# Delta-rule chains in four parts per step, and an output projection that starts on its attention half

## The chip, the core and the metric

One core of a Trainium2 chip runs the kernel. The metric is device time in microseconds (us) of one execution; the time of a kernel is the median of several runs. One execution was also taken by the hardware profiler, and every row of a trace below is from it.

## What is computed

The kernel is one encoder block on 1024 tokens plus 16 meta tokens, width 1024. Two head groups work side by side on the same normalised input, and one output projection joins them; an MLP follows. What the change touches is the recurrence of the first group and the join:

```python
def step(S, xs):                                   # per chunk, per direction, 4 heads
    q_i, k_i, u_i, w_i, qk_i, gl_i = xs
    v_new = u_i - einsum('bhck,bhkv->bhcv', w_i, S)
    o_i = einsum('bhck,bhkv->bhcv', q_i, S) + einsum('bhij,bhjv->bhiv', qk_i, v_new)
    S = S * gl_i[..., None, None] + einsum('bhck,bhcv->bhkv', k_i, v_new)
    return S, o_i
...
o = rms_norm(o_f + o_b, o_norm_w) * silu(heads(z))
mix = concatenate([o_dn, o_at], axis=-1) @ w_out[l]
h = h + rms_norm(mix, norm_mix_post[l])
u = rms_norm(h, norm_mlp_pre[l])
f = square(relu(u @ w_up[l])) @ w_down[l]
```

The second group is softmax attention with 8 query heads over all tokens.

## The kernel before

**Stages.** Input projections and the triangular inverses of the delta rule fill the first 400 us. Then three things share the engines: the two chains of the delta rule (one forward, one backward over 8 chunks of 128 tokens, `chain`, L1065), attention (8 tiles of 128 queries, 8 heads each, so 64 heads), and the output projection with its norms (`proj_stream`, L1387, 8 tiles). After that come the MLP's two products, each written as seven products of half-size blocks.

**A chain's step.** For a chunk c and four heads: the state times the keys (`st,KT`), eviction to `rr` on VectorE (DVE, L1078); the inverse times it (`rr,tt`), eviction to `vn`, which is `rr` again (L1090); the queries times the state (`st,QT`), eviction to `O` on ScalarE (ACT, L1097), and for a chunk that the other direction has already visited a sum with its stored output `Oprev` on GpSimd (POOL, L1099); `rr,kd`, whose eviction makes the next state (L1107); and `rr,at`, which DVE adds to `O` (L1113). `Oprev` is loaded from `oscr` in DRAM. The four operands of the next chunk (`vt`, `tt`, `kd`, `at`, 256 KB each) are loaded with `chunk_load` as soon as the step has used the old ones. All matrix products of a chain are float32, 128 x 128.

**A head of attention.** Four products of 512 columns into `S`, a minimum on DVE (L1254), the exponential on ACT (L1262), a cast (L1268) and the rest of the split on POOL and DVE (L1270, L1271) into `P`, one DMA transpose from `P` to `pT` (L1274, 128 x 16 x 128 values of two bytes) issued by SyncE's queue (SP), and 24 products `o<-VP,pT` (27 with a share of the meta tokens). At most six heads are between their scores and their products.

**The projection.** `mix(c)` transposes a tile of attention (`AQ`) and of the delta rule (`on`) and splits both; 96 products follow in the order `WORD`: first the attention rows of the weight (`woah`, `woal`), then the delta rule's (`wobh`, `wobl`). The first four are loaded by `wload_stream`, the others by `wout_stream` (L1334), which has to wait for both chains, because it takes over their memory.

**What sets the order.** Every stream is a Python generator. `progress` (L1538) runs the first stream of the list `URGENCY` whose due time has come on a planned clock, which counts TensorE's columns. After a `yield` a stream is due again its `LAT` later (2.2 us for the chains), or after the number of microseconds that it yields. `need` holds a stream until other streams have set a mark. So a `yield` between two parts of a chain's step puts 2.2 us of other streams' work between them. All this only fixes the order; the Tile framework then lays the instructions out, and each engine runs its own list in order, each instruction with its waits.

Of the kernel before, what the change touches and what calls it, by code (L numbers as in the profile page):

```python
# [13 lines left out]
ALU = mybir.AluOpType  # L14
AX = mybir.AxisListType
P = 128
# [65 lines left out]
def body(tc, I, out, dbg=None):  # L82
# [32 lines left out]
    def psr():  # L115
        return psa.tile([P, 512], F32, name="a", tag="a")
# [10 lines left out]
    def bc(ap, m):  # L127
        return ap.unsqueeze(2).broadcast_to([ap.shape[0], ap.shape[1], m])
# [4 lines left out]
    def v3(ap, m=P):  # L133
        return ap.rearrange("p (h c) -> p h c", c=m)
# [918 lines left out]
    def chunk_load(d, c, names):  # L1053
        if 0 <= c < NT:
            for n_ in names:
                loaded[n_, d] = t = ct_(f"{n_}{d}")
                S.dma_start(t, vscr[c * P:(c + 1) * P, :] if n_ == "vt" else {"at": dscr, "kd": kscr, "tt": tscr}[n_][d * NT + c])

    def ct_(name):

        if name not in R:
            R[name] = R["chn"].tile([P, 512], F32, name=name)
        return R[name]

    def chain(d, c, nxt):  # L1065
        gc = c * 8 + d * 4
        st = state[d]
        QT = R["QT"]
        tt, at, kd, vt = (loaded[n_, d] for n_ in ("tt", "at", "kd", "vt"))
        qc = [QT[:, h, c * P:(c + 1) * P] for h in range(NH)]  # L1070
        first = c not in seen
        seen.add(c)
        ps = psr()
        for h in range(NH):
            T.matmul(v3(ps)[:, h], lhsT=kcol(h, c), rhs=v3(st)[:, h], start=True, stop=True)
        rr = ct_(f"rr{d}")
        for h in range(NH):
            V.scalar_tensor_tensor(v3(rr)[:, h], v3(ps)[:, h], Egc[:, d, c, h:h + 1], v3(vt)[:, h], ALU.mult, ALU.subtract)  # L1078
        yield
        chunk_load(d, nxt, ("vt",))  # L1080
        if not first:
            yield from need(f"o{c}")
            prev = ct_(f"Oprev{d}")
            S.dma_start(prev, oscr[c])
        yield
        ps = psr()
        for h in range(NH):
            T.matmul(v3(ps)[:, h], lhsT=v3(tt)[:, h], rhs=v3(rr)[:, h], start=True, stop=True)
        vn = rr
        V.tensor_tensor(v3(vn), v3(ps), bc(nbeta[:, gc:gc + 4], P), ALU.mult)  # L1090
        yield
        ps = psr()
        for h in range(NH):
            T.matmul(v3(ps)[:, h], lhsT=qc[h], rhs=v3(st)[:, h], start=True, stop=True)
        oq = ct_(f"O{d}")
        for h in range(NH):
            A.activation(v3(oq)[:, h], v3(ps)[:, h], AF.Copy, scale=Egc[:, d, c, h:h + 1])  # L1097
        if not first:
            G.tensor_tensor(oq, oq, prev, ALU.add)  # L1099
        chunk_load(d, nxt, ("tt",))  # L1100
        yield
        ps = psr()
        for h in range(NH):
            T.matmul(v3(ps)[:, h], lhsT=v3(kd)[:, h], rhs=v3(vn)[:, h], start=True, stop=True)
        sg = ct_(f"st{d}{nxt % 2}")
        for h in range(NH):
            V.scalar_tensor_tensor(v3(sg)[:, h], v3(st)[:, h], Egl[:, d, c, h:h + 1], v3(ps)[:, h], ALU.mult, ALU.add)  # L1107
        state[d] = sg
        yield
        ps = psr()  # L1110
        for h in range(NH):
            T.matmul(v3(ps)[:, h], lhsT=v3(at)[:, h], rhs=v3(vn)[:, h], start=True, stop=True)
        V.tensor_tensor(oq, oq, ps, ALU.add)  # L1113
        chunk_load(d, nxt, ("kd",))
        yield
        chunk_load(d, nxt, ("at",))
        if first:
            S.dma_start(oscr[c], oq)
            mark(f"o{c}", 2.0)
            return  # L1120
        so = small(NH, "so", 2)
        jk = junk()
        for h in range(NH):
            A.activation(jk[:, :P], v3(oq)[:, h], AF.Square, accum_out=so[:, h:h + 1])
        mo = small(NH, "mo", 2)
        V.tensor_scalar(mo, ssq[:, c], P * EPS, P * EPS * EPS, ALU.mult, ALU.add)
        V.scalar_tensor_tensor(mo, so, 1.0 / P, mo, ALU.mult, ALU.add)
        ro = small(NH, "ro", 2)
        G.tensor_tensor(ro, mo, mhalf[:, :NH], ALU.pow)
        G.tensor_tensor(v3(oq), v3(oq), bc(ro, P), ALU.mult)  # L1130
        yield
        S.dma_start(oscr[c], oq)
# [193 lines left out]
    def wout_raw(k, r):  # L1326
        S.dma_start(r, w_out[k * P:(k + 1) * P, :])
        return r
# [5 lines left out]
    def wout_stream():  # L1334
        yield from need("chain0", "chain1", "wload")
        right.close()
        rkt.close()
        w3 = R["w3"] = pool(right, "w3", 2, side="right")
        wob = [w3.tile([P, 4, D], F32R, name=n, bufs=1) for n in ("wobh", "wobl")]
        R["npost"] = w3.tile([P, D], F32, name="npost", bufs=1)  # L1340
        R["npre"] = w3.tile([P, D], F32, name="npre", bufs=1)
        R["dnw"] = w3.tile([P, 1], F32, name="dnw", bufs=1)
        raw = [wout_raw(k, R[("npost", "npre")[k]] if k < 2 else tmp()[:, :D]) for k in range(4)]
        yield 4.0
        for k in range(4):
            wout_split(wob[0][:, k], wob[1][:, k], raw[k])
            yield
        R["wout"] = {k: tuple(a[:, k % 4] for a in (wob, R["wo"])[k // 4]) for k in range(KD)}
        S.dma_start(R["dnw"], I["dn_out_norm"][0].rearrange("(p o) -> p o", o=1))
        S.dma_start(R["npost"], I["norm_mix_post"][0].partition_broadcast(P))  # L1350
        S.dma_start(R["npre"], I["norm_mlp_pre"][0].partition_broadcast(P))
        mark("wout", 2.0)
        yield 4.0
        mx, su, isu = (w3.tile([P, 1], F32, name=n, bufs=1) for n in ("gmx", "gsu", "isu0"))
        R["isu"] = isu
        V.tensor_reduce(mx, R["npre"], AX.X, ALU.max, apply_absolute_value=True)
        V.tensor_scalar(mx, mx, 1e-30, None, ALU.max)
        pow2_below(mx, isu, su, 2.0 ** 7)
        V.tensor_scalar(R["npre"], R["npre"], su[:, 0:1], None, ALU.mult)
        mark("gain", 1.0)  # L1360
# [3 lines left out]
    def mix(c):  # L1364
# [19 lines left out]
        V.tensor_tensor(ml[:, 0:4], on, mh[:, 0:4].bitcast(F32), ALU.subtract)  # L1384
        return mh, ml

    def proj_stream():  # L1387
        mixes = {}
        yield from need("wout", "att0")
        mixes[0] = mix(0)  # L1390
        yield
        wout, npost = R["wout"], R["npost"]
        for c in range(NT):
            if c + 1 < NT:
                yield from need(f"att{c + 1}")
# [6 lines left out]
            for n in range(2):  # L1402
                sl = slice(n * 512, (n + 1) * 512)
                pso.append(psr())
                yield from mm3(pso[n], [(mh[:, k], ml[:, k], wout[k][0][:, sl], wout[k][1][:, sl]) for k in WORD], 2)
                A.activation(junk()[:, sl], pso[n], AF.Square, accum_out=s2[:, n:n + 1])
                yield
            rs = small(1, "rs")
# [482 lines left out]
```

## Time and profile before

| | us |
|---|---|
| median of 3 runs (1413.14 to 1415.83) | 1415.37 |
| the profiled execution, its own time | 1416.07 |
| its span, first to last instruction | 1414.2 |
| PE busy (TensorE's products), share of the span | 1342.7, 95% |
| DVE busy | 1029.3, 73% |
| ACT busy | 835.5, 59% |
| POOL busy | 295.4, 21% |
| mean granted clock of TensorE, as a share of 2.4 GHz | 0.979 |

PE is TensorE, PEld its weight loads. A busy share of 95% says little by itself, since a product counts as busy from its issue to its modelled end and these overlap; the profile has to be read stage by stage. The profile's second part, the span in 40 slices, shows PE below nine tenths only between some 400 and 810 us, and there the DMA engines are at nine tenths or more for most of the slices. That is the stage of chains, attention and projection. Rows with "<-" name what an engine waited for; "SPq" is SyncE's queue, which issues nearly all DMAs.

### The profile page before, as it was taken

Reading aid. Unit: us, or ns where it says so; the run is one execution under the profiler, and the core shown is the slowest. Engines: PE = TensorE matmul, PEld = TensorE weight load, DVE = VectorE, ACT = ScalarE, POOL = GpSimd, SP = SyncE. Lnnn points to the kernel's source line nnn. Section 1 sums busy time; section 2 is a strip of 40 time slices with the busy share of each in tenths; the row PEclk is TensorE's granted clock in tenths of the full one; section 3 lists DMA queues with packets and bytes.
Section 4 is the critical chain, followed back from the end, with each engine's and each line's share of the span. In section 5 each row is a group of like instructions: output and inputs, shape, how many; then the busy total and the mean of one; then the engine's idle time right before and its main releaser. Section 6 shows DMA issues by size and latency. Waiting matters only on the chain. (4 is left out here: it accounts for less than half of the span.)

```text
span 1414.2 us, 26476 instructions
## 1 busy us (share of the span) xinstructions
PE 1342.7 (95%) x9627; PEld 1027.1 (73%) x9627; DVE 1029.3 (73%) x1962; ACT 835.5 (59%) x1747; POOL 295.4 (21%) x386
## 2 busy tenths in 40 slices
PE   6999999999998998899998799999999999999996
PEld 6999888777998877677777444444444888888875
DVE  5636779788768979877765987777775588675675
ACT  6556565756546777866644676666665455445552
POOL 1210234343534456533321200000000000000000
PEclk9999999999998999889999799999999999999998
DMA  6312234344379999997994354444443984466341
GB/s 209 87 57 62 83 98 158 112 149 153 121 253 282 245 264 239 221 242 186 224 225 135 102 175 158 153 155 150 158 155 114 331 271 127 142 193 194 98 150 66
DMA packets 273355, 236.86 MB, mean 167 GB/s; under 512 B 147484, under 2 KB 201656, under 8 KB 273224
## 3 DMA queue, kind: packets, MB, share of 16 engines
q1 hardware_dynamic: 270056, 225.73, 55.3%
q10 hardware_dynamic: 3168, 9.44, 1.8%
q8 instruction: 76, 1.25, 0.4%
q14 instruction: 55, 0.45, 0.1%
HBM read 132.27 MB, written 69.28 MB: 143 GB/s over the span
## 5 line engine op out<-in xcount | busy, mean ns | idle before, releaser
L95 PEld LDWEIGHTS <-wh 128*128 128x128 f16 x896 | 88.1, 99 | 102.7 <-issue 1.9
L95 PE MATMUL a<-woah 128*128 128x512 f32 x672 | 158.6, 390 | 1.3 <-DVE woah L1734 1.2
L95 PE MATMUL a<-woal 128*128 128x512 f32 x672 | 157.4, 389 | 0.0
L95 PEld LDWEIGHTS a<-woah 128*128 128x128 f32 x672 | 125.9, 188 | 29.0 <-DVE woah L1734 2.0
L95 PEld LDWEIGHTS a<-woal 128*128 128x128 f32 x672 | 126.1, 188 | 26.2
L95 PE MATMUL a<-uh,wh 128*128 128x344 f32 (+2 forms) x340 | 122.3, 360 | 0.7 <-ACT cw L665 0.5
L1270 POOL TENSOR_TENSOR P<-t,P 128x640 f16<-128x640 f32 x64 | 99.4, 1555 | 106.8 <-ACT P L1268 85.0
L95 PE MATMUL a<-ul,wh 128*128 128x344 f32 (+2 forms) x340 | 118.7, 349 | 0.5 <-DVE ul L262 0.5
L95 PE MATMUL a<-uh,wl 128*128 128x344 f32 (+2 forms) x340 | 118.3, 348 | 0.0
L161 POOL TENSOR_TENSOR rs<-ms,mhalf 128x1 f32<-128x1 f32 (+1 forms) x33 | 19.1, 578 | 424.0 <-DVE rs L1797 304.6
L1254 DVE TENSOR_REDUCE mx<-S 128x1 f32<-128x1024 f32 x64 | 77.9, 1219 | 24.3 <-PE S L95 24.1
L1262 ACT ACTIVATE t<-S,nb 128x1024 f32<-128x1024 f32 x64 | 71.5, 1117 | 40.8 <-DVE nb L1255 29.2
L95 PEld LDWEIGHTS <-pT 128*128 128x128 f16 x1536 | 59.5, 100 | 42.0 <-issue 26.6
L95 PE MATMUL o<-VP,pT 128*128 128x65 f16 (+1 forms) x1536 | 73.6, 198 | 11.3 <-DMA pT<-P 9.8
L95 PEld LDWEIGHTS <-wl 128*128 128x128 f16 x448 | 43.9, 98 | 54.1 <-issue 1.7
L1731 ACT ACTIVATE woah<-fr,isf 128x512 fp32r<-128x512 f32 x54 | 39.2, 725 | 70.3 <-PE a L95 61.0
L1731 ACT ACTIVATE woal<-fr,isf 128x512 fp32r<-128x512 f32 x54 | 39.2, 726 | 68.4 <-PE a L95 66.2
L1268 ACT CAST P<-t 128x1024 f16<-128x1024 f32 x64 | 66.8, 1043 | 4.7 <-DVE t L269 1.8
L1733 DVE SCALAR_TENSOR_TENSOR woah<-fr,isf,woah 128x512 fp32r<-128x512 f32 x54 | 40.5, 751 | 37.2 <-ACT woah L1731 37.1
L95 PE MATMUL S<-KH,qs 128*128 128x512 f32 x128 | 61.0, 476 | 6.5 <-ACT t L1262 6.5
L95 PEld LDWEIGHTS a<-uh,wh 128*128 128x128 f32 x340 | 65.0, 191 | 2.5 <-ACT cw L665 0.7
L95 PEld LDWEIGHTS a<-ul,wh 128*128 128x128 f32 x340 | 65.1, 192 | 2.1 <-DVE ul L262 1.0
(508 smaller groups left out, 3776.8 us busy)
## 6 DMA issues: line engine op xcount, KB each, us to landing
fr<-fscr SPq DMA_DIRECT2D x108, 256.0 KB
fscr<-os SPq DMA_DIRECT2D x64, 256.0 KB
rb<-in_w_down SPq DMA_DIRECT2D x64, 256.0 KB
fscr<-of SPq DMA_DIRECT2D x48, 256.0 KB
wr<-in_w_in SPq DMA_DIRECT2D x44, 256.0 KB
AQ<-in_w_up SPq DMA_DIRECT2D x22, 512.0 KB
raw<-in_w_up SPq DMA_DIRECT2D x10, 512.0 KB
X<-in_x SPq DMA_DIRECT2D x8, 512.0 KB
```

Source lines behind the costliest of these rows:

```text
L95: nc.tensor.matmul(out, lhsT=lhsT, rhs=rhs, **kw)
L161: G.tensor_tensor(dst, ms[:r, :n], mhalf[:r, :n], ALU.pow)
L1254: V.tensor_reduce(mx, s, AX.X, ALU.min)
L1262: A.activation(p32[:, :L], s, AF.Exp, bias=nb, scale=-1.0)
L1268: A.copy(p16[:, 0], p32[:, :L])
L1270: G.tensor_tensor(p16[:, 1, :LH], p32[:, :LH], p16[:, 0, :LH], ALU.subtract)
L1731: A.activation(ah, fr, AF.Copy, scale=isf[:, p:p + 1])
L1733: V.scalar_tensor_tensor(al, fr, isf[:, p:p + 1], ah.bitcast(F32), ALU.mult, ALU.subtract)
```

## The change

It does three things. A chain's step has two `yield`s fewer: the one behind the loads of the first part and the one ahead of the last part's loads are gone, so that a step has four parts, `KT`, `tt`, `kd` with `QT`, and `at` (a chunk's second visit has a fifth, its norm). The product with the queries moves behind the state's update, into the same part. The loads move with them: `tt` and `kd` are now issued in the part that has used them, and `Oprev` is asked for after `vn` and no longer after `rr`. And the output projection waits at first for `w3` only (the weights' pool is open and their loads are issued), and for `wout` ahead of the delta rule's half of the products.

```diff
--- before.py
+++ after.py
@@ -1076,19 +1076,27 @@
         rr = ct_(f"rr{d}")
         for h in range(NH):
             V.scalar_tensor_tensor(v3(rr)[:, h], v3(ps)[:, h], Egc[:, d, c, h:h + 1], v3(vt)[:, h], ALU.mult, ALU.subtract)
-        yield
         chunk_load(d, nxt, ("vt",))
-        if not first:
-            yield from need(f"o{c}")
-            prev = ct_(f"Oprev{d}")
-            S.dma_start(prev, oscr[c])
         yield
         ps = psr()
         for h in range(NH):
             T.matmul(v3(ps)[:, h], lhsT=v3(tt)[:, h], rhs=v3(rr)[:, h], start=True, stop=True)
         vn = rr
         V.tensor_tensor(v3(vn), v3(ps), bc(nbeta[:, gc:gc + 4], P), ALU.mult)
-        yield
+        chunk_load(d, nxt, ("tt",))
+        if not first:
+            yield from need(f"o{c}")
+            prev = ct_(f"Oprev{d}")
+            S.dma_start(prev, oscr[c])
+        yield
+        ps = psr()
+        for h in range(NH):
+            T.matmul(v3(ps)[:, h], lhsT=v3(kd)[:, h], rhs=v3(vn)[:, h], start=True, stop=True)
+        sg = ct_(f"st{d}{nxt % 2}")
+        for h in range(NH):
+            V.scalar_tensor_tensor(v3(sg)[:, h], v3(st)[:, h], Egl[:, d, c, h:h + 1], v3(ps)[:, h], ALU.mult, ALU.add)
+        state[d] = sg
+        chunk_load(d, nxt, ("kd",))
         ps = psr()
         for h in range(NH):
             T.matmul(v3(ps)[:, h], lhsT=qc[h], rhs=v3(st)[:, h], start=True, stop=True)
@@ -1097,22 +1105,11 @@
             A.activation(v3(oq)[:, h], v3(ps)[:, h], AF.Copy, scale=Egc[:, d, c, h:h + 1])
         if not first:
             G.tensor_tensor(oq, oq, prev, ALU.add)
-        chunk_load(d, nxt, ("tt",))
-        yield
-        ps = psr()
-        for h in range(NH):
-            T.matmul(v3(ps)[:, h], lhsT=v3(kd)[:, h], rhs=v3(vn)[:, h], start=True, stop=True)
-        sg = ct_(f"st{d}{nxt % 2}")
-        for h in range(NH):
-            V.scalar_tensor_tensor(v3(sg)[:, h], v3(st)[:, h], Egl[:, d, c, h:h + 1], v3(ps)[:, h], ALU.mult, ALU.add)
-        state[d] = sg
         yield
         ps = psr()
         for h in range(NH):
             T.matmul(v3(ps)[:, h], lhsT=v3(at)[:, h], rhs=v3(vn)[:, h], start=True, stop=True)
         V.tensor_tensor(oq, oq, ps, ALU.add)
-        chunk_load(d, nxt, ("kd",))
-        yield
         chunk_load(d, nxt, ("at",))
         if first:
             S.dma_start(oscr[c], oq)
@@ -1340,13 +1337,14 @@
         R["npost"] = w3.tile([P, D], F32, name="npost", bufs=1)
         R["npre"] = w3.tile([P, D], F32, name="npre", bufs=1)
         R["dnw"] = w3.tile([P, 1], F32, name="dnw", bufs=1)
+        R["wout"] = {k: tuple(a[:, k % 4] for a in (wob, R["wo"])[k // 4]) for k in range(KD)}
+        S.dma_start(R["dnw"], I["dn_out_norm"][0].rearrange("(p o) -> p o", o=1))
         raw = [wout_raw(k, R[("npost", "npre")[k]] if k < 2 else tmp()[:, :D]) for k in range(4)]
+        mark("w3")
         yield 4.0
         for k in range(4):
             wout_split(wob[0][:, k], wob[1][:, k], raw[k])
             yield
-        R["wout"] = {k: tuple(a[:, k % 4] for a in (wob, R["wo"])[k // 4]) for k in range(KD)}
-        S.dma_start(R["dnw"], I["dn_out_norm"][0].rearrange("(p o) -> p o", o=1))
         S.dma_start(R["npost"], I["norm_mix_post"][0].partition_broadcast(P))
         S.dma_start(R["npre"], I["norm_mlp_pre"][0].partition_broadcast(P))
         mark("wout", 2.0)
@@ -1384,12 +1382,23 @@
         V.tensor_tensor(ml[:, 0:4], on, mh[:, 0:4].bitcast(F32), ALU.subtract)
         return mh, ml
 
+    def proj_mm(ps, mh, ml, sl):
+
+        for i, k in enumerate(WORD):
+            if i == 4:
+                yield from need("wout")
+            wh, wl = (w[:, sl] for w in R["wout"][k])
+            for j, (a, b) in enumerate(((mh, wh), (mh, wl), (ml, wh))):
+                T.matmul(ps, lhsT=a[:, k], rhs=b, start=i == 0 and j == 0, stop=i == KD - 1 and j == 2)
+            if i % 2 and i + 1 < KD:
+                yield
+
     def proj_stream():
         mixes = {}
-        yield from need("wout", "att0")
+        yield from need("w3", "att0")
         mixes[0] = mix(0)
         yield
-        wout, npost = R["wout"], R["npost"]
+        npost = R["npost"]
         for c in range(NT):
             if c + 1 < NT:
                 yield from need(f"att{c + 1}")
@@ -1402,7 +1411,7 @@
             for n in range(2):
                 sl = slice(n * 512, (n + 1) * 512)
                 pso.append(psr())
-                yield from mm3(pso[n], [(mh[:, k], ml[:, k], wout[k][0][:, sl], wout[k][1][:, sl]) for k in WORD], 2)
+                yield from proj_mm(pso[n], mh, ml, sl)
                 A.activation(junk()[:, sl], pso[n], AF.Square, accum_out=s2[:, n:n + 1])
                 yield
             rs = small(1, "rs")
```

**On TensorE, chains.** The chains' second step before and third step with the change, in both the place where the last input projections run out (`st` is a state, `rr` with `tt`, `kd`, `at` the other products, `idr`, `KM` the first query tile; forward and backward have different numbers). Before:

```order
L95 MATMUL a<-rr_5956,tt_5764 128x128 x4
L95 MATMUL a<-rr_5966,tt_5774 128x128 x4
L95 MATMUL a<-idr,t_6263 128x128 x8
L95 MATMUL a<-st_6153,QT 128x128 x4
L95 MATMUL a<-st_6163,QT 128x128 x4
L95 MATMUL a<-KM,qs 128x32 x8
L95 MATMUL a<-rr_5956,kd_5766 128x128 x4
L95 MATMUL a<-rr_5966,kd_5776 128x128 x4
```

With the change:

```order
L95 MATMUL a<-rr_5956,tt_5764 128x128 x4
L95 MATMUL a<-rr_5967,tt_5774 128x128 x4
L95 MATMUL a<-rr_5956,kd_5766 128x128 x4
L95 MATMUL a<-st_5758,QT 128x128 x4
L95 MATMUL a<-rr_5967,kd_5776 128x128 x4
L95 MATMUL a<-st_5768,QT 128x128 x4
L95 MATMUL a<-rr_5956,at_5762 128x128 x4
L95 MATMUL a<-st_6060,KT 128x128 x4
L95 MATMUL a<-rr_5967,at_5772 128x128 x4
L95 MATMUL a<-st_6081,KT 128x128 x4
```

The chains' products now follow each other with nothing between them; `kd` stands right behind `tt` and `QT` behind `kd`. Over the whole stage the two lists, counted in products, compare as follows:

| in TensorE's list, counted from the chains' first product | before | change |
|---|---|---|
| products up to the chains' last one | 1429 | 661 |
| of these, heads' scores / heads' products with `pT` | 35 / 29 | 12 / 6 |
| from there to the projection's first product | 369 | 376 |
| heads' scores / heads' products still to come at that point | 18.5 / 24.0 | 41.5 / 46.8 |
| products of the projection after the last head's | 96 | 91 |

**On SyncE's queue, the end of the chains.** Before, from the last chain stores on:

```order
L1132 DMA oscr<-O_6109 128x512
L1327 DMA t_8730<-in_w_out 128x1024
L1327 DMA t_8732<-in_w_out 128x1024
L1327 DMA npost<-in_w_out 128x1024
L1327 DMA npre<-in_w_out 128x1024
L1274 DMA_TRANSPOSE pT<-P_6215 128x16x128
L1274 DMA_TRANSPOSE pT<-P_6216 128x16x128
```

With the change:

```order
L1129 DMA oscr<-O_6092 128x512
L1324 DMA t_7512<-in_w_out 128x1024
L1271 DMA_TRANSPOSE pT<-P_6380 128x16x128
L1341 DMA dnw<-in_dn_out_norm 128x1
L1324 DMA npost<-in_w_out 128x1024
L1324 DMA npre<-in_w_out 128x1024
L1367 DMA zt<-zscr 128x4x128
L1369 DMA on<-oscr 128x512
L1271 DMA_TRANSPOSE pT<-P_6377 128x16x128
```

The first tile's `zt` and `on` now stand directly behind the weights' loads. Only 11 of the 64 transposes stand ahead of the first of these four loads (34 before).

## Rows read from the trace of the kernel before

**Rows 1.** Stretches: window and length, busy us of PE, PEld, DVE, ACT, POOL; granted clock; DMA share; GB/s.

```profile
400.00:624.00 224.00, 200.45 (x2136) 175.98 (x2136) 184.92 (x400) 157.87 (x347) 107.91 (x85) 0.92 1.04 252
624.00:745.00 121.00, 116.61 (x1054) 89.16 (x1053) 78.93 (x140) 67.95 (x118) 38.53 (x31) 1.00 0.89 212
745.00:775.00 30.00, 28.57 (x169) 23.48 (x166) 18.01 (x38) 12.36 (x28) 5.25 (x7) 1.00 0.49 153
```

**Rows 2.** Tiles' instructions, ns min/median/max, first and last start: chains, projection, attention.

```profile
L95 PE MATMUL a<-rr,at x128: 270/275/377, 418.2 to 582.7; 128*128 128x128 f32 x128
L95 PE MATMUL a<-woah,mh x64: 388/394/502, 623.7 to 770.4; 128*128 128x512 f32 x64
L95 PE MATMUL o<-VP,pT x1536: 190/194/278, 455.5 to 745.2; 128*128 128x65 f16 x128, 128*128 128x64 f16 x64
```

**Rows 3.** What SyncE's transposes waited for, 402 to 775 us: us in total, times, longest.

```profile
SPq L1274 <- POOL P L1270: 62.8, 30, 5.1
SPq L1274 <- PE o L95: 35.6, 20, 3.8
```

**Rows 4.** Prices of transfers: stretch 402 to 420; DMA 449 to 616; SyncE's issues.

```profile
402.00:420.00 18.00, 18.00 (x158) 17.95 (x157) 10.71 (x34) 9.11 (x42) 5.46 (x6) 1.00 0.75 265
...
DMA packets 93132, 40.78 MB, mean 244 GB/s; under 512 B 84425, under 2 KB 84532, under 8 KB 93109
pT<-P SPq DMA_TRANSPOSE x41
...
L1274 SPq DMA_TRANSPOSE pT<-P x64: 1577/2545/6613, 449.1 to 730.1; - x64
592.61 15.54 SPq L1274 DMA_TRANSPOSE pT<-P  x5
```

**Rows 5.** DMA of the stretches 400 to 583 and 583 to 624 us.

```profile
DMA packets 81648, 46.51 MB, mean 254 GB/s; under 512 B 67925, under 2 KB 68821, under 8 KB 81625
pT<-P SPq DMA_TRANSPOSE x32
...
DMA packets 22133, 9.99 MB, mean 244 GB/s; under 512 B 19744, under 2 KB 20768, under 8 KB 22129
pT<-P SPq DMA_TRANSPOSE x10
```

**Rows 6.** PE in order of time: start us, us; a chain's product is two instructions.

```profile
401.84 1.95 PE L95 MATMUL a<-st,KT 128*128 128x128 f32 x16
403.54 0.37 PE L95 MATMUL a<-wh,uh 128*128 128x256 f32 x1
...
744.23 0.39 PE L95 MATMUL a<-wobh,ml 128*128 128x512 f32 x1
744.46 0.90 PE L95 MATMUL o<-VP,pT 128*128 128x65 f16 x24
745.20 0.22 PE L95 MATMUL o<-VM,pmh 128*128 128x65 f16 x2
```

**Rows 7.** Groups by line, 402 to 583 us: count, busy us, mean ns, idle before.

```profile
L1270 POOL TENSOR_TENSOR P<-t,P 128x640 f16<-128x640 f32 x34 | 52.7, 1553 | 40.9 <-ACT P L1268 31.0 <-issue 8.0 <-DMA pT<-P 1.1
L1254 DVE TENSOR_REDUCE mx<-S 128x1 f32<-128x1024 f32 x34 | 41.3, 1217 | 13.3 <-PE S L95 13.2
L1097 ACT ACTIVATE O<-a,dec 128x128 f32<-128x128 f32 x64 | 17.9, 381 | 8.0 <-PE a L95 5.8 <-POOL P L1270 1.7 <-PE S L95 0.3
L1107 DVE SCALAR_TENSOR_TENSOR st<-st,dec,a 128x128 f32<-128x128 f32 x64 | 17.7, 341 | 1.3 <-PE a L95 1.1
L1090 DVE TENSOR_TENSOR rr<-a,nbeta 128x512 f32<-128x512 f32 x16 | 10.8, 683 | 1.4 <-PE a L95 1.3
L1099 POOL TENSOR_TENSOR O<-O,Oprev 128x512 f32<-128x512 f32 x8 | 10.1, 1273 | 8.4 <-ACT O L1097 8.4
```

**Rows 8.** Stretches of 5 us around a chain's wait, columns as in Rows 1.

```profile
420.00:425.00 5.00, 2.30 (x19) 1.92 (x17) 5.00 (x12) 0.00 (x0) 0.66 (x5) 1.00 0.93 295
425.00:430.00 5.00, 4.81 (x26) 4.81 (x27) 3.81 (x11) 1.48 (x3) 1.96 (x2) 0.66 0.95 308
```

More of the change, by code (lines that the diff above doesn't have):

```diff
@@ L1078, in chain @@
             V.scalar_tensor_tensor(v3(rr)[:, h], v3(ps)[:, h], Egc[:, d, c, h:h + 1], v3(vt)[:, h], ALU.mult, ALU.subtract)
+        chunk_load(d, nxt, ("vt",))
         yield
-        chunk_load(d, nxt, ("vt",))
+        ps = psr()
+        for h in range(NH):
+            T.matmul(v3(ps)[:, h], lhsT=v3(tt)[:, h], rhs=v3(rr)[:, h], start=True, stop=True)
+        vn = rr
+        V.tensor_tensor(v3(vn), v3(ps), bc(nbeta[:, gc:gc + 4], P), ALU.mult)
+        chunk_load(d, nxt, ("tt",))
         if not first:
@@ L1087, in chain @@
         for h in range(NH):
-            T.matmul(v3(ps)[:, h], lhsT=v3(tt)[:, h], rhs=v3(rr)[:, h], start=True, stop=True)
-        vn = rr
-        V.tensor_tensor(v3(vn), v3(ps), bc(nbeta[:, gc:gc + 4], P), ALU.mult)
-        yield
+            T.matmul(v3(ps)[:, h], lhsT=v3(kd)[:, h], rhs=v3(vn)[:, h], start=True, stop=True)
[4 more added lines that the diff above has]
+        chunk_load(d, nxt, ("kd",))
         ps = psr()
```

## The prediction

> **What bounds the kernel now.** I read the stretches first, and in them the share of the DMA engines beside that of TensorE. From 400 to 624 us, where chains and attention run, PE is busy 200 of 224 us at a granted clock of 0.92 of 2.4 GHz, while the DMA engines are full (share 1.04). From 624 to 745 us, with the projection added, it is the other way round: PE is busy 117 of 121 us at full clock, and the DMA share is 0.89 [rows 1]. So one stage has two limits in turn, transfers first and products afterwards. The tiles' rows give the borders: the chains' last product starts at 582.7, the projection's first at 623.7, the heads' last at 745.2, the projection's last at 770 us [rows 2]. The waits of SyncE's queue show how the two meet: transposes wait 62.8 us for POOL's part of `P` and 35.6 us for PE to give `pT` back [rows 3], so a late head delays its transfer, and a late transfer its products.
>
> Neither limit's total work is changed. What changes is which work lies in which stretch: before, 34 heads' transposes are issued during the chains and 24 heads are left for the projection's stretch; with the change 11 and 46.8. The question is whether the transfer-bound stretch shortens by more than the product-bound one grows.
>
> **Price of a transfer.** Between 402 and 420 us no transpose runs: 265 GB/s at a share of 0.75, so 353 GB/s or 2.83 us per MB when full [rows 4]. Between 449 and 616 us the engines are full: 40.78 MB, of which 41 transposes of 0.524 MB are 21.5 MB. The 19.3 MB of copies take 54.6 us, and the other 112.4 of 167 us make 2.74 us per transpose. The bounds are SyncE's median issue, 2.55 us, and five transposes in a row in 15.54 us, 3.1 us each [rows 4].
>
> **First stretch, up to the projection's first product.** Before, 46.51 + 9.99 MB with 42 transposes [rows 5] are 34.5 MB of copies, 97.6 us, and 115.1 us of transposes: 212.7 of 224 us, 95%. With the change the copies stay, 35 MB with one more tile's inputs, 99 us. At the projection's first product 17 heads are multiplied and 22.5 scored, so about 20 are transposed: 55 us. That is 154 us, at the same 95% 162 us: the projection begins at about **562** us, 62 us earlier. Bounds by the transposes' price: 558 to 570 us.
>
> Is PE fast enough for that? Sixteen instructions of a chain's product take 1.70 us to the next one [rows 6], so one product 0.2125 us, and a step's 40 (both directions) 8.5 us, eight steps 68 us. A product of 512 columns starts every 0.23 us, and 24 with `pT` take 0.74 us, 0.031 each [rows 6]; a head is thus 0.92 + 0.84 us, with its share of the query tile's 16 products about 2.2 us. 20 heads and 9 us of the last input projection make 121 us of 162. DVE needs, per step of both directions, 8 instructions of 0.34 us for the state and 8 of the same kind for `rr`, two of 0.68 for `vn` and two of that size for `O` [rows 7]: at most 8.2 us, and 66 us in all. Neither is the limit over the stretch, though in the steps without attention PE's 8.5 and DVE's 8.2 us leave nothing spare.
>
> **The loads that moved.** `tt` and `kd` are asked for in the part that uses the old ones. They are still a step ahead, and eight loads and two stores are 2.6 MB, 7.4 us of transfers in a step of at least 8.5. I put them at nothing; the cover is the other direction's products. Without it a load's 0.74 us stands in the chain, 12 us for 16 visits. `Oprev` is asked for one part later; that is the rival below.
>
> **Second stretch, to the last head's product.** Before: 116.6 us of PE for 24 heads. The projection's products are nearly the same (293 against 288). 22.8 more heads at 2.2 us are 50 us: 166.6 us. Its idle 4.4 us, scaled by heads, become 8.6: **175** us instead of 121. The transfers fit: 44 transposes, 121 us, and the stretch's 25.66 MB less 23 transposes, 13.6 MB or 38 us, are 159 us. A bound from above: 89% PE, as in the first stretch before [rows 1], gives 187 us; from below no idle, 167.
>
> **What lies behind.** The projection's products behind the last head are 91 instead of 96, and the list is the same from there on: 0 us, between -1 for the five and +1. The earlier start on the attention half costs and gives nothing by itself: the first products wait for the second tile of attention, when the weights' second half has long been split.
>
> **Sum.** 562 + 175 = 737 against 745 us: 8 us earlier. The profiled execution took 1416.07 us, 0.7 above the median; 1416 - 8 = **1408** us.
>
> **Rivals.**
>
> *Faster: the transposes are cheaper than they look.* If they cost 2.07 us where the engines leave them room, halfway between SyncE's shortest issue, 1.58, and its median [rows 4], the account is 99 + 41 = 140, at 95% 147 us; then the projection begins at 547 and the time is 1393. For it: the share goes beyond 1, so packets wait on each other and the price is inflated. Against it: with nearly no copies beside them, five took 3.1 us each. The Trainium skill, "DMA: Bandwidth & Descriptors", section "Latency and other measured facts", gives 261 GB/s for DMA transposes in one kernel; as an estimate that is 2.0 us for 0.524 MB, and the time would be the 1393 of this rival. The trace, with 2.74 us, does not agree so far.
>
> *The projection's stretch has two limits at once, and nothing is gained.* There PE needs 167 us and the transfers 159. DVE's 79 us [rows 1] become 131 with 22.8 more heads at 2.3, an estimate of nearly twice the 1.2 us of the minimum [rows 7]. Before, only PE was full there. At 92% PE the stretch takes 181 us and the time is 1414; at 91% it is 1416, no change.
>
> *Slower: DVE stands still for POOL in each second visit.* Before, a part with the state's update lies between `QT` and `at`. Now the chain ACT (four of 0.38, 1.1 us start to end), POOL's sum (1.27 us) [rows 7] and `Oprev` have only the other direction's 12 products, 2.55 us, before DVE comes to its sum. DVE waits in order, with the other direction's `rr` and the heads' minima behind it, and PE behind those. POOL is also busy with 1.55 us per head, and a load from DRAM stands behind transposes of 2.7 us in SyncE's list. A wait like that has a second price: after 2.7 us of idle PE the clock was at 0.66 for the next 5 us [rows 8], so that PE's spare quarter goes too. With 2.5 us in each of eight visits, 20 us, the first stretch takes 182 us, an efficiency of 85%, and the time is 1428. It decides from 1 us a visit: 8 us eat the whole gain. Against it: the chains' evictions on DVE waited little before, 1.1 to 1.4 us in all per line [rows 7], and part of the stops falls into time in which only transfers count.
>
> *The change does not compress the chains,* because their loads come late: the step stays at the 22.6 us of before. Then nothing moves, and the time is 1416; the list of TensorE speaks against it.
>
> **Chances.** About 0.2% (2.8 us) is what a measurement of this kernel can tell from no change; no change is 1412.6 to 1418.2 us. Forecast (1400 to 1412): 0.43. Cheaper transposes: 0.13. Two limits or no compression: 0.18. DVE behind POOL, or a second stretch at 89% PE: 0.26. So faster 0.56, same 0.18, slower 0.26. The second stretch's bound of 187 us would be 1420. The range reaches from the faster rival, 1393, to the slower one, 1428.
>
> **What would show it.** Right: the chains' last product near 520 us and the projection's first near 562; a DMA share above 1 up to there; from there PE above 94% at full clock with 3.7 us per head; the last head's product near 737. Wrong, in the first term: a start of the projection after 572, with DVE's `O` sum or PE's `rr`, `st` waiting for POOL or ACT. Wrong in the second: a stretch above 183 us with PE waiting for `pT`, or for DVE. If the stretch between the chains' end and the projection is longer than the 41 us of before, the transposes that the chains kept waiting have been pushed there.

## The result, and the profile after

The change makes the kernel **slower: 1449.72 us** (median of 4 runs, 1445.3 to 1451.5) against 1415.6 us (1413.14 to 1417.66), a ratio of 1.0228 with a 95% interval of 1.0207 to 1.025. The forecast was 1408, with 1428 as the end of its range.

The borders of the stage come first, from the tiles of the kernel after, in the columns of [rows 2]:

```profile
L95 PE MATMUL a<-rr,at x128: 270/275/423, 415.2 to 526.3; 128*128 128x128 f32 x128
L95 PE MATMUL a<-woah,mh x64: 387/394/776, 572.8 to 802.1; 128*128 128x512 f32 x64
L95 PE MATMUL o<-VP,pT x1536: 190/194/278, 476.3 to 780.4; 128*128 128x65 f16 x128, 128*128 128x64 f16 x64
```

The chains end at 526.3 instead of 582.7 us, so they are compressed as the change says. The projection begins at 572.8 instead of 623.7 us, 51 us earlier. The heads' last product, however, comes at 780.4 instead of 745.2 us, 35 us later: the stretch between the two takes 207.6 us, where it took 121.5. The span, 1447.6 against 1414.2 us, is 33.4 longer, so that the loss is all made by then.

The stretches of the kernel after, in the columns of [rows 1]:

```profile
400.00:480.00 80.00, 73.47 (x612) 70.61 (x611) 60.60 (x157) 36.18 (x118) 20.41 (x21) 0.98 0.84 281
400.00:527.00 127.00, 114.73 (x1017) 108.20 (x1016) 99.86 (x247) 69.38 (x208) 53.35 (x47) 0.96 0.93 272
527.00:573.00 46.00, 30.68 (x364) 25.12 (x363) 35.74 (x62) 32.21 (x57) 21.96 (x17) 0.81 1.04 222
573.00:780.00 207.00, 179.73 (x1820) 135.98 (x1820) 133.08 (x240) 125.72 (x206) 72.82 (x55) 0.96 0.80 184
780.00:802.00 22.00, 22.00 (x138) 18.09 (x135) 11.54 (x21) 9.93 (x21) 3.62 (x4) 1.00 0.52 171
```

The row to read is the fourth. In the projection's stretch neither limit is full: PE is busy 87% of the time at a clock of 0.96 (before 96% at 1.00 [rows 1]), and the DMA share is 0.80 (before 0.89). Slices of 5 us, picked out of that stretch, show one reason why both averages are below full:

```profile
600.00:605.00 5.00, 3.07 (x15) 1.79 (x13) 5.00 (x13) 4.73 (x7) 2.19 (x3) 1.00 0.93 267
615.00:620.00 5.00, 5.00 (x43) 3.69 (x42) 1.91 (x3) 2.91 (x6) 1.73 (x1) 1.00 0.47 107
635.00:640.00 5.00, 3.92 (x50) 2.87 (x47) 3.71 (x6) 3.08 (x4) 1.95 (x2) 1.00 1.14 316
645.00:650.00 5.00, 5.00 (x30) 3.69 (x29) 1.73 (x3) 2.29 (x4) 1.99 (x2) 0.74 0.25 87
675.00:680.00 5.00, 3.21 (x22) 2.07 (x21) 4.88 (x7) 4.76 (x8) 3.27 (x3) 1.00 1.17 305
695.00:700.00 5.00, 4.59 (x54) 3.53 (x52) 2.81 (x5) 3.42 (x6) 1.41 (x1) 1.00 0.36 79
```

Stretches in which PE is full or nearly so and the DMA engines stand at a quarter to a half (615, 645, 695) alternate with stretches in which the DMA engines are full and PE has gaps (600, 635, 675). The alternation is not clean. Of the 41 such slices from 575 to 780 us, 15 have gaps in PE at a DMA share of 0.8 or more, eight have PE full at a lower share, in ten both are full, and in eight neither is. Over slices of 20 us PE is busy 14.2 to 19.6 us from 620 to 760 us in the kernel after, and 18.5 to 19.8 us from 640 to 740 us in the kernel before.

What SyncE's queue waited for between 573 and 780 us in the kernel after, in the columns of [rows 3]:

```profile
SPq L1271 <- PE o L95: 71.8, 27, 6.2
SPq L1271 <- DVE P L1268: 22.6, 15, 4.1
SPq L1271 <- POOL P L1267: 16.1, 9, 2.5
```

and the same in the kernel before, between 624 and 745 us:

```profile
SPq L1274 <- PE o L95: 24.0, 15, 3.0
SPq L1274 <- POOL P L1270: 21.1, 10, 5.1
```

The transposes now wait 71.8 us, up to 6.2 at a time, for PE to give one of the three `pT` buffers back. PE holds them while it runs projection products; when these are used up, the heads follow one another as fast as the transposes let them, and PE waits. What ended PE's own waits between 573 and 780 us (four of the five largest), in the same columns:

```profile
PE o L95 <- DMA pT<-P: 8.0, 8, 1.8
PE a L99 <- DVE AQ L1307: 5.4, 4, 2.5
PE S L95 <- ACT t L1259: 3.5, 5, 1.0
PE o L95 <- DVE AQ L1307: 2.7, 1, 2.7
```

Of PE's 27.3 idle us, only 8.0 end directly with a transpose, and 8.1 end with DVE's `AQ`, the output of attention's heads. In four of those five waits (5.4 us) it is the projection that stands, at the transposes of an attention tile that DVE has only just finished. Between 624 and 745 us in the kernel before, PE waited for neither; most of its waiting there, 3.8 us, was for `t` (L1414).

### The profile page after: what moved, and what is told of

It reads as the page before. It is cut to its first block, busy times and chain, and to the rows that moved or that the text cites. A ratio compares the mean times of both kernels' runs of the same rounds, so it can differ in the third digit from the quotient of the medians.

```text
span 1447.6 us, 26448 instructions
## 1 busy us (share of the span) xinstructions
PE 1348.6 (93%) x9627; PEld 1030.4 (71%) x9627; DVE 1030.7 (71%) x1962; ACT 835.6 (58%) x1747; POOL 295.2 (20%) x386
## 5 line engine op out<-in xcount | busy, mean ns | idle before, releaser
L95 PE MATMUL o<-VP,pT 128*128 128x65 f16 (+1 forms) x1536 | 76.1, 202 | 25.4 <-DMA pT<-P 18.5
```

Source lines behind the costliest of these rows:

```text
L95: nc.tensor.matmul(out, lhsT=lhsT, rhs=rhs, **kw)
```

## The experiments

The theory after this reading (A): chains that end early let the projection begin early, it then catches up with attention, and runs in bursts that shut the transposes out. The rivals: the early start on the attention half costs (B); the dense or rearranged chains themselves lose time (C, F below); the totals of TensorE and the transfers cost this much in any order (D); three buffers for `pT` are too few (E); the heads that dense chains leave for afterwards cost, whatever the projection does (P).

Of the line `LAT`, the table of pauses, the edits below show only the entry that changes; "..." marks lines left out.

**First question: which of the two parts of the change costs?** The chains alone: of the change only the part in `chain`, nothing of the projection's.

```diff
-        yield
         chunk_load(d, nxt, ("vt",))
...
+        chunk_load(d, nxt, ("tt",))
...
     def proj_stream():
         yield from need("wout", "att0")
```

> The kernel before with the four-part chains alone; the projection still waits for the whole converted weight. Theory A (the projection catches up with attention because the chains end 56 us earlier, so that it runs in bursts that shut the transposes out; the half start adds little to that): the chains' last tile near 526 us, the second stretch (projection's first product to the last head) still near 200 us, time 1435 to 1452. Theory B (the early start of the projection with its attention half is what costs): the loss goes away, at most 1416, as my account of transfers and products has it, and near 1405 if that account was right. Theory C (the denser chains lose time themselves): the loss stands before the projection's first product, not behind it.

Measured: 1453.77 us, ratio 1.0244 (1.0218 to 1.0269). The chains end at 526.5, the projection begins at 578.0, the last head is at 786.4 us: the whole loss, in the same stretch (208.4 us), and 2 us above the range expected by theory A. Theory C has fallen, since the projection begins early and the loss stands behind its start. The other part alone, `chain` as before and the projection as after:

```diff
...
     def proj_stream():
-        yield from need("wout", "att0")
+        yield from need("w3", "att0")
...
```

> The kernel after with the chains of before (seven parts), so the early start of the projection alone. Theory A: the chains still end near 583 us and leave a backlog of finished tiles, so nothing to catch up with: within 0.3% of before, 1411 to 1420. Theory B: most of the loss is here, 1440 or more. Theory C: no loss, as A.

Measured: 1413.07 us, ratio 0.9969 (0.9951 to 0.9987), a little faster than the kernel before. The projection begins at 603.9 instead of 623.7 us. So theory B has fallen, and the early start alone is a gain of some 4 us.

**Second question: is it the form of the four parts, or that they lie close together?** Form and spacing can be crossed, since the planner's pause between parts is a number. The kernel after, spaced:

```diff
-chain=2.2
+chain=3.85
```

> The kernel after with the planner's pause between a chain's parts set from 2.2 to 3.85 us, so that four parts a step are planned as far apart, in all, as seven were (15.4 us a step). Theory P (it is the chains' density that costs: the queries' heads are what keeps the transfers busy beside chain products, and chains done in 111 us leave 45 of the 64 transposes for afterwards, where TensorE and the transfers take turns): the chains' last tile moves back to about 575 to 585 us and the time returns to 1408 to 1420. Theory F (the four-part form itself costs, its waits and the moved loads): 1440 or more. Theory A alone (the projection catching up) asks for the same as P here, since the backlog is restored too.

Measured: 1415.53 us, ratio 0.9986 (0.997 to 1.0002); the chains end at 569.0 us, a little ahead of the expected 575 to 585. And the seven parts of before with the projection of after, set close:

```diff
-chain=2.2
+chain=1.26
```

> The kernel after with the chains of before, in seven parts, but the pause between parts set from 2.2 to 1.26 us, so that a step is planned as short as the four-part step (8.8 us). Theory P: the chains end earlier than 583 us, the more so the more the loss of the kernel after returns: 1430 to 1455 if they end by 540 us. Theory F: no loss, 1408 to 1418 as with the chains of before.

Measured: 1445.73 us, ratio 1.0205 (1.0181 to 1.0229), chains' end 532.1 us. So seven and four parts cost the same at the same spacing, 1413 and 1416 spaced, 1446 and 1450 dense; the order inside a step, the moved loads and the later `Oprev` cost nothing that shows. Theory F has fallen. The tiles of the four parts spaced, as above:

```profile
L95 PE MATMUL a<-rr,at x128: 270/275/377, 418.5 to 569.0; 128*128 128x128 f32 x128
L95 PE MATMUL a<-woah,mh x64: 388/397/773, 595.0 to 770.3; 128*128 128x512 f32 x64
L95 PE MATMUL o<-VP,pT x1536: 190/193/278, 455.8 to 748.7; 128*128 128x65 f16 x128, 128*128 128x64 f16 x64
```

**Third question: why do dense chains cost behind their end?** The projection can be held until a backlog lies ready:

```diff
-yield from need("w3", "att0")
+yield from need("w3", "att4")
```

> The kernel after, but the projection's first tile waits until tile 4 of attention is done, so that a backlog of finished tiles lies ready as in the kernel before. Theory A: from then on the projection fills between the heads in small pieces, the waits of the transposes for a buffer that is held behind projection's products fall to the 24 us of before or less, time 1418 to 1430. Theory D (TensorE's and the transfers' totals in that stretch cost this much in any order): still 1445 to 1452, as the same work stands in the same span.

Measured: 1434.26 us, ratio 1.0119 (1.0102 to 1.0135); the last head is at 761.7 us. Above the expected range by 4 us, but far from 1450. The transposes' waits for PE fell to 28.1 us in 13 waits from 646 to 762 us, where at most 24 were expected. Stretches of this kernel, without the projection (to 646) and with it:

```profile
580.00:646.00 66.00, 55.48 (x749) 44.61 (x748) 55.78 (x92) 53.81 (x83) 31.27 (x22) 0.92 0.89 178
646.00:762.00 116.00, 111.40 (x998) 84.92 (x995) 80.51 (x133) 64.57 (x113) 36.58 (x29) 1.00 0.87 209
```

With the backlog, PE is at 96% and full clock again, as before the change; what is lost lies now ahead of it, where heads run without filler at 84% PE. The same projection products can instead be spread thinner:

```diff
-proj=0.18
+proj=0.9
```

> The kernel after with the projection's cost in the order's table set from 0.18 to 0.9 us a piece, which spreads its pieces over five times as much of the other work. Theory A: the bursts of up to 16 products a head thin out, TensorE stays filled between the heads, 1420 to 1437. Theory D: 1445 to 1452, no change beyond 0.3%. If the wait for the next tile, and not the size of the bursts, is what costs, this does nothing while the hold to tile 4 gains.

Measured: 1431.66 us, ratio 1.01 (1.0067 to 1.0134). In its projection's stretch, with chains just as dense and as many heads left, PE and the DMA engines are both fuller than in the kernel after:

```profile
575.00:764.00 189.00, 173.44 (x1814) 130.48 (x1813) 139.47 (x232) 123.48 (x201) 71.69 (x54) 0.97 0.87 196
```

Nearly the same work stands in 189 instead of 207 us, so theory D has fallen. The opposite end, the heads entirely without the projection:

```diff
-yield from need("w3", "att0")
+yield from need("w3", "att7")
```

> The kernel after with the projection held until the last tile of attention, so that the heads run alone and the projection alone behind them: the price of a head without filler. From the stretch without projection in the kernel held to tile 4 (22.3 heads in 66 us, 2.96 us a head): 46 heads behind the chains take about 136 to 146 us, the last head's product near 690 to 705 us; then the projection's 384 products at 0.23 us are 88 us more, the last near 785 to 800 us, and the time 1425 to 1445. If heads can go at TensorE's 2.2 us alone, the last one is at about 660 and the time below 1410.

Measured: 1463.42 us, ratio 1.0327 (1.0301 to 1.0354), above the range. The heads came out as expected, with the last one at 704.0 us:

```profile
573.00:701.00 128.00, 101.84 (x1492) 79.38 (x1490) 107.95 (x180) 104.90 (x156) 62.63 (x44) 0.97 0.97 185
701.00:826.00 125.00, 110.87 (x513) 88.30 (x512) 55.38 (x101) 35.33 (x80) 14.32 (x19) 0.92 0.45 153
...
573.00:701.00 128.00, 46.77 (x1104) 39.33 (x1102) 0.97 0.97 185
```

The last row counts the products with `pT` alone: 1104, 24 a head, are 46 heads in 128 us, **2.78 us a head without filler**, at a DMA share of 0.97. TensorE's work for a head was 2.2 us. What I missed is the second row: the projection alone took 125 us, where I had 88 from its products. PE stands still for 14.1 of them (12.0 us are waits for `t` at L1423), the granted clock of 0.92 is some 10 us by itself, an estimate, and the rest is products that the 88 left out, the transposes of the `mix` tiles among them. Alone, each of the two streams leaves PE gaps that the other can fill.

A fourth buffer for `pT`, paid for with one of the four for `P`:

```diff
-INF, P16N = 6, 4
+INF, P16N = 6, 3
-AB, GB, SB, PTB = 3, 5, 2, 3
+AB, GB, SB, PTB = 3, 5, 2, 4
```

> The kernel after with four buffers for the transposed probabilities instead of three, at the price of three instead of four for the probabilities before the transpose (there is no room for both). Theory E (the transposes stand for a buffer behind projection's products, 71.8 us in 27 waits, and that is the loss): a third of those waits goes and the time falls by 8 to 20 us, 1430 to 1442. If the waits only move to the probabilities' buffers, or the bursts last longer than one more buffer covers: 1445 to 1455.

Measured: 1443.4 us, ratio 1.0189 (1.0164 to 1.0213), at the border between the two expectations. The waits of its queue from 573 to 780 us:

```profile
SPq L1271 <- DVE P L1268: 51.1, 25, 4.9
SPq L1271 <- POOL P L1267: 31.7, 19, 3.1
SPq L1271 <- PE o L95: 16.0, 11, 3.0
```

The wait for PE fell from 71.8 to 16.0 us, and those for `P` rose from 38.7 to 82.8: most of the stop moved one buffer up. Not all of it: the stretch from the projection's first product to the last head took 195.7 us instead of 207.6, though 6.5 us of this were lost again because the projection began later. So theory E holds for a part of the loss: the number of buffers is part of the price of a change-over. More buffers of both kinds at once were not tried.

**Fourth question: how does the loss depend on the spacing?**

```diff
-chain=2.2
+chain=3.0
```

> The kernel after with the pause between a chain's parts at 3.0 us, about halfway between 2.2 (1449) and 3.85 (1416). Theory P, the loss grows with what the chains leave for afterwards: the chains' last tile near 550 us and 1425 to 1438. A threshold instead of a slope would give 1414 to 1420 or 1445 to 1452.

Measured: 1446.94 us, ratio 1.0213 (1.0187 to 1.0238). Not the slope: halfway in spacing, the loss is still nearly whole. And wider:

```diff
-chain=2.2
+chain=5.0
```

> The kernel after with the pause at 5.0 us, the chains spread wider than in the kernel before (20 us a step). If spreading goes on to help: 1400 to 1412. If the chains now end late and the projection, which waits for the second tile's queries' output behind them, has nothing left to hide behind: 1418 to 1435. The slope from 2.2 to 3.85 alone would say 1393; I expect the second.

Measured: 1431.97 us, ratio 1.0107 (1.0077 to 1.0138): the chains end at 617.8 and the projection begins at 642.8 us, too late. The tiles of the kernel at 3.0:

```profile
L95 PE MATMUL a<-rr,at x128: 270/275/377, 418.4 to 547.0; 128*128 128x128 f32 x128
L95 PE MATMUL a<-woah,mh x64: 387/397/776, 572.0 to 801.5; 128*128 128x512 f32 x64
L95 PE MATMUL o<-VP,pT x1536: 190/194/278, 463.1 to 779.9; 128*128 128x65 f16 x128, 128*128 128x64 f16 x64
```

The chains end 21 us later than in the kernel after, and the two other borders are the same. So I counted, in the order of TensorE's instructions, how many projection products stand beside each head from the projection's start to the last head. In the kernel after the counts run

```
24 12 12 0 0 0 0 12 12 12 12 0 0 0 0 12 12 12 12 0 0 0 0 ...
```

A tile's projection is 48 products (384 for 8 tiles; the 96 in the description above are two tiles'), 12 beside each of four heads, and then nothing beside the next four, because the projection of tile c waits for attention's tile c + 1 and a tile has eight heads. The projection eats tiles twice as fast as attention makes them. With H heads done at its start, the H/8 tiles, less the two that the first needs, last for H - 16 heads. The kernel before starts with 40 heads done and 24 left: 40 - 16 = 24, **exactly to the last head**. The kernel after starts with 17: the backlog lasts for one head, and half of the other 45 go bare (25 counted). At 3.0 us it is 21, so five heads and half of 38 bare (22 counted); at 3.85 us 30, so 14 heads and half of 20 (9 counted). That fits 2.2 and 3.0 being alike and 3.85 not. Two more spacings of the kernel after test it:

```diff
-chain=2.2
+chain=3.4
```

> Four parts, pause 3.4 us; in the order 25 heads are done at the projection's start and 16 of the remaining 39 have no projection product beside them. If the time follows the bare heads (1446.9 at 22, 1415.5 at 9, so 2.4 us each): 1426 to 1438. If it is a threshold in the chains' end: 1444 to 1450 or 1412 to 1419.

Measured: 1440.88 us, ratio 1.0154 (1.0129 to 1.0178): between the rows on either side, but above the expected slope and below the expected plateau.

```diff
-chain=2.2
+chain=4.4
```

> Four parts, pause 4.4 us; 35 heads done at the projection's start, 6 of the remaining 29 bare. By the bare heads alone 1408; but at 5.0, with 4 bare, it was 1432, since the projection started at 643 us: between, 1408 to 1424.

Measured: 1424.73 us, ratio 1.0043 (1.0028 to 1.0058), just above the upper end.

All kernels but the one with the projection behind the heads (the three with wider pauses and the thinner half start are those of the last question), with the excess of the projection's stretch: its length less 2.2 us for each head left and 0.23 us for each projection product issued by the last head (288 in the kernel before, 293 in that after, 228 to 293 in all), both prices from before the change.

| kernel | chains' end | projection's start | last head | heads left | bare | excess us | median us |
|---|---|---|---|---|---|---|---|
| before | 582.7 | 623.7 | 745.2 | 24 | 2 | 2 | 1415.6 |
| half start alone | 581.3 | 603.9 | 743.8 | 29.5 | 7 | 9 | 1413.1 |
| half start, thinner projection | 582.2 | 605.7 | 737.1 | 29 | 7 | 15 | 1417.9 |
| half start, pause 2.3 | 589.4 | 615.3 | 750.8 | 27 | 3 | 10 | 1425.3 |
| half start, pause 2.4 | 592.4 | 621.0 | 745.9 | 25 | 2 | 4 | 1419.9 |
| half start, pause 2.6 | 606.5 | 630.8 | 738.9 | 22 | 3 | 5 | 1421.9 |
| four parts, pause 5.0 | 617.8 | 642.8 | 746.7 | 21 | 4 | 2 | 1432.0 |
| four parts, pause 4.4 | 593.1 | 618.1 | 755.2 | 28.7 | 6 | 8 | 1424.7 |
| four parts, pause 3.85 | 569.0 | 595.0 | 748.7 | 34 | 9 | 11 | 1415.5 |
| four parts, pause 3.4 | 561.4 | 584.4 | 775.6 | 39 | 16 | 38 | 1440.9 |
| four parts, pause 3.0 | 547.0 | 572.0 | 779.9 | 43 | 22 | 46 | 1446.9 |
| after (pause 2.2) | 526.3 | 572.8 | 780.4 | 46.7 | 25 | 37 | 1449.7 |
| chains alone | 526.5 | 578.0 | 786.4 | 46.7 | 25 | 38 | 1453.8 |
| after, four `pT` buffers | 529.8 | 579.3 | 775.0 | 45.9 | 26 | 28 | 1443.4 |
| seven parts dense | 532.1 | 577.7 | 779.8 | 44 | 19 | 38 | 1445.7 |
| after, held to tile 4 | 523.9 | 646.6 | 761.7 | 21.7 | 4 | 4 | 1434.3 |
| after, thin projection | 525.7 | 574.7 | 764.2 | 47 | 10 | 21 | 1431.7 |

Up to nine bare heads the excess is 2 to 11 us, but 15 with the half start and a thinner projection; from sixteen on it is 37 to 46, but 28 with a fourth `pT` buffer. The last row is the cleanest one: chains, projection's start and heads left nearly as in the kernel after, and the same projection in smaller portions beside more heads, so that the bare heads go from 25 to 10. 16 us of excess are gone. That is theory A's share as far as it is shown, about half of the loss. Whether the other half would go too if no head were bare, or belongs to the heads left over (P), no run separates. The median does not follow the excess alone, since a stretch that begins later ends later: the pauses of 5.0 and 4.4 have little excess and are slow.

**Is there something faster than both?** Four more attempts with the chains of before and the half start, one with a thinner projection, three with wider pauses:

```diff
-proj=0.18
+proj=0.4
```

> The chains of before with the half start, and the projection's cost in the order's table set from 0.18 to 0.4 us. A candidate to be faster than both. With a backlog of finished tiles the projection already lies evenly between the heads, so theories A and P expect little: 1405 to 1418.

Measured: 1417.85 us, ratio 1.0007 (0.9994 to 1.002).

```diff
-chain=2.2
+chain=2.3
```

and the same with 2.4 and with 2.6:

> The chains of before in seven parts with the half start, pause 2.3 us: 37 heads done at the projection's start, 3 of 27 bare (7 of 30 at 2.2, which gave 1413). By the bare heads 4 to 8 us better than that: 1404 to 1412; by the later start of the projection alone, about 1415 to 1418.

> As the one before with pause 2.4 us: 39 heads done, 2 of 25 bare, the backlog lasting almost exactly to the last head. 1405 to 1418; 2.6 gave 1422.

> The chains of before in seven parts with the half start, and a pause of 2.6 instead of 2.2 us (18 us a step). Candidate to be faster than both: 1403 to 1418.

Measured: 1425.26 us, ratio 1.0046 (1.0029 to 1.0063); 1419.92 us, ratio 0.9999 (0.9984 to 1.0014); 1421.94 us, ratio 1.0037 (1.0023 to 1.0051). All three lie above what was expected. The first is the clearest miss: only 3 bare heads by the count, yet an excess of 10 us and a time that is worse than both of its neighbours, 2.2 and 2.4. The count of bare heads separates large losses from small ones; it does not order kernels that lie within 12 us of one another, and what sets those stays open. The best kernel of all is the half start alone, 0.3% faster than before.

## Why the prediction was wrong

**The chains (right).** Forecast near 520 us, 526.3 came. PE is busy 114.73 of the first 127 us there.

**The first stretch, 562 us (mis-sized by 11).** The prices fit, the efficiency of 95% did not. The kernel after moves 44.75 MB between 400 and 573 us, with 19 transposes:

```profile
DMA packets 56940, 44.75 MB, mean 259 GB/s; under 512 B 40211, under 2 KB 42643, under 8 KB 56920
pT<-P SPq DMA_TRANSPOSE x19
```

By the prediction's prices these are 34.8 MB of copies, 98.5 us, and 52.1 us of transposes, 150.6 of 173 us or 87%. The DMA share fell with it, from 1.04 to 0.96. The lost share is at the beginning: from 400 to 480 us the DMA share is 0.84, against 0.95 in the kernel before (PE is busy 73 of these 80 us in both), because PE's time goes to the dense chains and the first head's product comes at 476.3 instead of 455.5 us. I carried a mean efficiency of a stretch in which transposes ran throughout over to one in which they start late. The start at 572.8 is what I had named as wrong for this term ("after 572"), though not for the reason named there: DVE's sum hardly waits for POOL. From the chains' end to the projection's start it is 46.5 us instead of 41, which was the sign for transposes pushed there.

**The second stretch, 175 us (the step that failed).** It took 207.6, beyond the 187 given as its bound from above. The prediction read: "Its idle 4.4 us, scaled by heads, become 8.6". PE's idle time is 27.3 us instead of 8.6, and its busy time 179.73 instead of 166.6; a mean clock of 0.96 over 207 us accounts for some 8 of these 13 us, an estimate; the other 5 stay open. The idle time of the kernel before was small because five finished tiles lay ready, so that all but two of the 24 heads had projection products beside them. Scaling it by heads took that for a property of the heads. The sign that was named for this, a stretch above 183 us with PE waiting for `pT` or for DVE, came true in both its forms: 8.0 us for the transposes and 8.1 for DVE's `AQ`, waits that PE did not have in the kernel before. Filled, a head with 12 products needs 2.2 + 12 x 0.23 = 5.0 us of PE and one transpose of 2.74, and the transfers stand still for the rest; bare, it needs 2.78 us of transfers and 2.2 of PE, and PE stands still. Four of each are 31.1 us a tile, eight evenly filled ones (2.2 + 6 x 0.23 = 3.58) 28.6. The kernel after takes 207.6 / 46.7 x 8 = 35.6 us, so the change-overs cost more than the halves themselves. What the runs show of that price is the clock, some 8 us over the stretch, and the buffers, since a fourth for `pT` took the excess from 37 to 28 us; how the rest divides is not shown.

That the transfers fit by their total, 159 us, was right and beside the point. Both totals fit, 167 and 159 of 207 us; they did not fit at the same time.

**The tail (nearly right).** Forecast 0, between -1 and +1: the last head comes 35.2 us later and the end 33.4 us later, so 1.8 us are gained behind it. That the early start on the attention half "costs and gives nothing by itself" was wrong: with the chains of before it moves the projection's start from 623.7 to 603.9 us and is worth some 4 us.

**The rivals.** *Two limits at once* was nearest, but it had the stretch at 91 to 92% with both limits near full; it had no alternation in it, and its price was 181 to 184 us. *DVE behind POOL*, the rival on the other side, did not decide. The waits of the kernel after on that line between 400 and 573 us:

```profile
DVE O L1112 <- POOL O L1107: 3.6, 3, 1.4
DVE O L1112 <- ACT qs L1226: 3.5, 1, 3.5
```

3.6 us in three waits, where 20 in eight were priced (with all of its waits for ACT, 8.5 us in five), and the four parts spaced show that the form costs nothing. The 2.7 us of idle PE that this rival tied to the clock [rows 8] were not one wait but two, of 0.87 and 2.02 us, the second reaching past 425 us. *Cheaper transposes:* heads without filler, with hardly any copies beside them, still took 2.78 us each at a DMA share of 0.97. The 2.0 us that I estimated from the figure in the Trainium skill, "DMA: Bandwidth & Descriptors", section "Latency and other measured facts", is not reached there. What the prediction itself held against this rival was misread: the five transposes in 15.54 us did not have "nearly no copies beside them". In that time the DMA engines moved 4.16 MB, of which the five are at most 2.62; by the price of copies that leaves some 2.2 us for each, an estimate. *No compression* fell with the chains' end. The range missed because each rival priced one mechanism inside the chains or a fuller limit, and none asked what fills TensorE between the heads once the projection has caught up.

## What to carry to other kernels

When two streams with different limits share a stage, the one with the spare work is the other's filler: before bringing a stream forward, count how long its backlog will last, not only whether the totals fit. Where the consumer runs faster than its producer (here a tile in four heads against eight), it must start late enough, or be thinned enough, to last to the producer's end. And an efficiency that was read in a mixed stretch belongs to the mixture; it can't be scaled with one of its parts.

## What was not expected of the hardware

The price of an alternation is more than its idle time; the prediction had a drop of the clock only in the chains, as part of a rival. In the kernel after, PE had waited 1.83 us for a transpose at 634.84 us and 2.46 us for DVE's `AQ` at 641.78 us; the burst of projection products that follows begins at half pace. PE in order of time, start and length in us, and the slice around the second wait, in the columns of [rows 1]:

```profile
634.84 0.90 PE L95 MATMUL o<-VP,pT 128*128 128x65 f16 x24 [1.83 <-DMA pT<-P]
...
641.78 0.69 PE L99 MATMUL a<-c_id,AQ 128*128 128x128 f32 x2 [2.46 <-DVE AQ L1307]
...
644.47 0.63 PE L95 MATMUL a<-woah,mh 128*128 128x512 f32 x1
644.89 0.63 PE L95 MATMUL a<-woal,mh 128*128 128x512 f32 x1
...
647.91 0.39 PE L95 MATMUL a<-woal,mh 128*128 128x512 f32 x1
648.14 0.40 PE L95 MATMUL a<-woah,ml 128*128 128x512 f32 x1
...
640.00:645.00 5.00, 3.22 (x17) 2.71 (x18) 4.78 (x10) 4.76 (x9) 2.54 (x2) 0.58 0.83 233
```

Until 647 us the products start 0.42 us apart, from 648 us on 0.23: the 1.2 GHz level and then the 2.4 GHz level. The granted clock is 1.00 from 635 to 640 us (PE busy 3.92 of 5 us), 0.58 in the next slice, which holds most of the second wait (3.22 of 5 us busy), and 0.74 from 645 to 650, although PE is busy for all of that. So PE is slowed just where it is the limit, and the mean clock of the stretch is 0.96 instead of 1.00.
